# Attention scores on two 64-row halves of TensorE's array, and a written order on all engines from the gate columns to the end of the attention

## Chip, cores and metric

One core of a Trainium2 chip. The time is the device time of one execution in microseconds. Names of engines: PE is TensorE (its weight loads are PEld), DVE is VectorE, ACT is ScalarE, POOL is GpSimd; SP issues most DMAs.

## What is computed

Two layers of a backbone over 1024 latent and 256 context tokens of 1024 channels. Layer 0 (recurrent heads beside Fourier groups) isn't touched. Layer 1 is multi-head latent attention with 16 heads; a head's queries and keys have 64 plain and 32 rotary dimensions, the rotary key is the same for all heads, and the 1024 latent queries see all 1280 keys:

```python
def attend(q, k, v):
    s = jnp.einsum('bqhd,bkhd->bhqk', q, k, preferred_element_type=jnp.float32) * ATTN_SCALE
    p = jax.nn.softmax(s, axis=-1).astype(v.dtype)
    return jnp.einsum('bhqk,bkhd->bqhd', p, v)
...
    q_l = jnp.concatenate([q_l[..., :QK_NOPE], apply_axial_rope(q_l[..., QK_NOPE:], cos, sin)], axis=-1)
    kr_l = apply_axial_rope(kr_l[:, :, None, :], cos, sin)[:, :, 0]
...
    o_l = blocked_attention(q_l, k_all, v_all).reshape(b_, s_, MLA_WIDTH)
    y_lat = (o_l * jax.nn.silu(g_l)) @ w_out
```

The result is the latent stream after a layer norm, `[1, 1024, 1024]` in float32.

## The kernel before

**Precision.** A product of float32 accuracy is made of three float32r products: each operand is split into `hi` and `lo` of 12 bits, and hi·hi, hi·lo and lo·hi are summed in PSUM (`mm3`, lines 90 to 92; `split`, lines 81 to 87, copies on one engine and subtracts on another). The probabilities times values (`po`) and the row sums are plain float32 products, each of which stands in the trace as two instructions.

**Gate columns** (lines 973 to 994). For each of eight blocks `m` of 128 channels, `in1g` is the product of the gate's weights with the normalised activations, 2 x 8 x 3 products of 512 columns, followed by a sigmoid (ACT) and a product (DVE). Between them, spread over 128 steps, stand the closures of `work`: the weights and rotated queries of heads 0 to 3 (`prep_quad`), the queries and keys of heads 0 and 1 (`prep_pair`), their maximum (`max_pass`) and the values (`prep_v`).

**Attention** (lines 1006 to 1131). Heads go in pairs `p` = 0 to 7, queries in halves of 512, keys in ten tiles `kt` of 128. One step (`attend`) computes for both heads the scores `s` (lines 1021 to 1023: three products over 96 or 97 rows; the 97th row of `Qh` holds the negated maximum of a query and meets ones in `Kh`), the exponential (ACT, line 1025) and the running row sum `ra` (POOL, line 1029). After key tiles 1, 3, 5, 7, 8 and 9 it multiplies up to two tiles of probabilities with values (`po`, line 1034): head `a` writes the column half `64a` of the array. `finish` sums `ra` over partitions (`rp`, line 1059, column halves too), inverts in four pieces (DVE, line 1066), multiplies with the gate and stores.

Beside pair `p`, the next pair is prepared: for odd `p + 1` from the weights at hand, for even `p + 1` after a new `prep_quad` of four heads, which is part of the same list of closures. `ra` in `prep_quad` is one rotation: a product `pra`, then a shuffle, three products or sums and two halves of a split on DVE. `qr` copies rotated queries into rows 64 to 95 of `Qh` and `Ql` (DVE, lines 933 and 934). `max_pass` (lines 951 to 967) makes 16 units of three products (512, 512 and 256 keys) with a maximum on DVE after each; `rows` transposes the maxima and a DMA on POOL's queue puts them into the 97th row of `Qh`. Beside pair 7 the output weights are scaled and split (`wo1_load`, lines 1102 to 1109).

**Order.** All this is traced in the order of the loops, but a scheduler then orders every engine's instructions by its own estimates of costs, so the instructions of a step may stand elsewhere. PSUM has eight banks: four for `m_ps` (maxima and preparation), three for `s_ps`, one for `o_ps`.

Of the kernel before, what the change touches and what calls it, by code (L numbers as in the profile page):

```python
# [13 lines left out]
F32 = mybir.dt.float32  # L14
# [26 lines left out]
PVG = {1: (0,), 3: (1, 2), 5: (3, 4), 7: (5, 6), 8: (7,)}  # L41
PVL = (8, 9)
DK = -1
# [11 lines left out]
MB = 4  # L55
SB = 3
# [3 lines left out]
def _body(ctx, tc, ap, out, dbg=None):  # L60
# [36 lines left out]
    # ---------------------------------------------------------------- constants  # L97
# [13 lines left out]
    # v = 8 softplus(-lambda): softplus(x) = max(x, 0) + log1p(exp(-|x|)),  # L111
    # log1p(e) = 2 atanh(e / (2 + e))
# [26 lines left out]
    # the channel DFT folded into the group weights  # L139
# [9 lines left out]
    # ---------------------------------------------------------------- adaLN  # L149
    # stationary: the silu of the two condition vectors, 32 columns (two used)  # L150
# [8 lines left out]
    # shift and scale of both layers, channel-major: [128, layer, stream, 16] (8 shift, 8 scale)  # L159
# [14 lines left out]
    def ada_units(src, row, nm):  # L174
        """products of one set of four column chunks, a k-tile at a time, summed in SBUF"""
# [25 lines left out]
    def ada_gate(row):  # L201
        # rows 32j + m: chunk j of (layer, half), stream m
# [8 lines left out]
    # layer 0 by quarters of the channels, so that the projection can start on the first  # L211
# [4 lines left out]
    def ada_part(h):  # L216
# [12 lines left out]
        # chunk 2 s + i of shift (s = 0) and scale (s = 1): channel block 2 h + i  # L229
# [82 lines left out]
    # ---------------------------------------------------------------- RG-LRU heads  # L312
# [78 lines left out]
    # x projections run one head pair ahead of the gates that use them  # L391
# [3 lines left out]
    nop = lambda: None  # noqa: E731  # L395
# [18 lines left out]
    # ---------------------------------------------------------------- Fourier channel groups  # L414
# [24 lines left out]
    def fourier(g, work=()):  # L439
        """input projection of one group, then the rest as closures"""  # L440
# [9 lines left out]
        # even and odd parts over the token index, halves 0 .. N/2 - 1  # L450
# [7 lines left out]
        # the latent stream once more about N/4, for even and for odd frequencies  # L458
# [6 lines left out]
        # columns: u_ctx[N/2], ev_lat[N/4] and the alternating sums of both streams  # L465
# [15 lines left out]
        def channel(n, f0, wt):  # L481
            # channel DFT, tokens onto partitions
# [10 lines left out]
        def small():  # L493
# [7 lines left out]
            # alternating terms and bias  # L501
# [13 lines left out]
        def seq(n, tn, nm):  # L515
            # even frequencies in the first half of the columns, odd ones in the second
# [27 lines left out]
        nop = lambda: None  # noqa: E731  # L544
# [29 lines left out]
    def y_load(t, p):  # L574
        """the first eight channel blocks of a token tile"""
# [15 lines left out]
    # ---------------------------------------------------------------- layer 0: output projection, norm  # L591
# [6 lines left out]
    def w1_load(k, p, tag, eh, el):  # L598
        """the small columns of layer 1's input projection, a k-tile"""
# [202 lines left out]
    for n, t in enumerate(TOKE):  # L802
# [8 lines left out]
        if n == WG:  # L811
            wg_load(0, S, G)
# [18 lines left out]
    def slots(p, i0):  # L831
        for i in (i0, i0 + 1):
# [5 lines left out]
            if i == 0:  # L838
                for t in range(NT):
                    G.tensor_copy(out=Kh[0][96:97, P * t : P * t + P], in_=one)  # L840
# [464 lines left out]
```

## Time and profile before

| | us |
|---|---|
| median of three runs | 1495.59 (1495.51 to 1504.29) |
| the profiled execution's own time (its span) | 1498.8 |
| of it up to the gate columns | 722 |
| gate columns | 109 |
| attention, pairs 0 to 6 | 501 |
| attention, pair 7, to the first product of the output projection | 69.5 |
| output projection | 97.3 |

The stretches are read from the timeline: first `in1g`, first `s`, end of pair 6, first `yf`. An engine's busy time counts its instructions, and a PE instruction's duration includes the time through the array; so PE's pace is read from the distance between starts. In the rows, `128*64` is rows times columns of the array in use, and `x8` stands for eight instructions merged into one line.

### The profile page before, as it was taken

What the parts mean: (1) busy time and instruction counts of PE and PEld (TensorE: products, weight loads), DVE (VectorE), ACT (ScalarE), POOL (GpSimd) and SP (SyncE); (2) the same over time, 40 slices, a digit from 0 to 9 for tenths busy, and PEclk for the clock granted to TensorE, in tenths of its full rate; (3) what the DMA queues carried; (4) which work ended last, traced back from release to release, by engine and by line L of the source; (5) the groups of instructions that cost most, each with busy time, mean ns of one, the idle gap of its engine ahead of it and who ended that gap; (6) DMA issues with size and microseconds to landing.
All of it is one profiled execution on the core that took longest, in us unless ns stands there. A gap on an engine that the chain in (4) does not pass through costs nothing.

```text
span 1498.8 us, 18430 instructions
## 1 busy us (share of the span) xinstructions
PE 1434.9 (96%) x6880; PEld 1040.1 (69%) x6880; DVE 1037.0 (69%) x1636; ACT 571.7 (38%) x840; POOL 706.4 (47%) x460
## 2 busy tenths in 40 slices
PE   6998999999999999999999999999999999998898
PEld 3776777778888788879888655655566556554586
DVE  4669778765765243348675769787977787779498
ACT  2276565665113221124321544443444334443110
POOL 1135434343212154213411676677667756689652
PEclk9999999999999999999999999999999989999999
DMA  8613233332304653310231101010100000022542
GB/s 302 229 52 107 99 105 109 109 102 85 111 29 147 211 168 115 119 37 26 95 106 50 60 15 43 15 32 22 36 15 15 29 14 15 15 71 71 181 135 91
DMA packets 63641, 127.05 MB, mean 85 GB/s; under 512 B 5304, under 2 KB 31160, under 8 KB 61248
## 3 DMA queue, kind: packets, MB, share of 16 engines
q1 hardware_dynamic: 60592, 117.82, 24.1%
q0 software_dynamic: 2528, 7.67, 1.4%
q8 instruction: 54, 0.88, 0.3%
q10 hardware_dynamic: 432, 0.39, 0.1%
q14 instruction: 35, 0.29, 0.1%
HBM read 101.14 MB, written 24.66 MB: 84 GB/s over the span
## 4 chain that ended last, share of the span: by engine, by line
PE 72%; DVE 20%; DMA 3%; issue 2%; ACT 2%; POOL 1%; SPq 0%; DVEq 0%; ACTq 0%; POOLq 0%
PE z L272 13%; PE y L651 10%; PE po L1034 8%; PE yf L1167 6%; PE mx L955 5%; PE s L1021 4%; PE s L1023 4%; PE s L1022 4%; PE in1g L92 2%; PE in1g L90 2%; PE in1g L91 2%; DVE xc L322 2%; DVE th L367 1%; DVE gate L372 1%; DVE ri L1066 1%
## 5 line engine op out<-in xcount | busy, mean ns | idle before, releaser
L1029 POOL TENSOR_TENSOR ra<-ra,p 128x512 f32<-128x512 f32 x256 | 351.4, 1399 | 96.2 <-ACT p L1025 95.8
L1025 ACT ACTIVATE p<-s 128x512 f32<-128x512 f32 x320 | 190.1, 597 | 249.9 <-PE s L1023 222.2
L956 DVE TENSOR_REDUCE m<-mx 128x1 f32<-128x512 f32 (+1 forms) x384 | 207.8, 591 | 55.1 <-PE mx L955 53.8
L272 PE MATMUL z<-uh,w0h 128*128 128x512 f32 (+1 forms) x576 | 150.0, 367 | 4.3 <-ACT uh L81 4.3
L87 POOL TENSOR_TENSOR w0l<-w,w0h 128x1024 fp32r<-128x1024 f32 x24 | 63.9, 2664 | 184.5 <-DVE w0h L83 126.4
L272 PE MATMUL z<-uh,w0l 128*128 128x512 f32 (+1 forms) x576 | 147.7, 362 | 0.0
L272 PE MATMUL z<-ul,w0h 128*128 128x512 f32 (+1 forms) x576 | 147.7, 362 | 0.0
L1021 PE MATMUL s<-Qh,Kh 97*128 97x512 f32 x320 | 132.5, 414 | 6.3 <-ACT p L1025 6.3
L1022 PE MATMUL s<-Ql,Kh 96*128 96x512 f32 x320 | 128.1, 400 | 0.0
L1023 PE MATMUL s<-Qh,Kl 96*128 96x512 f32 x320 | 128.1, 400 | 0.0
L955 PE MATMUL mx<-Kh,Qh 96*128 96x512 f32 (+1 forms) x384 | 115.8, 376 | 7.9 <-DVE Ql L87 4.3
L272 PEld LDWEIGHTS z<-uh,w0h 128*128 128x128 f32 x576 | 98.4, 190 | 33.4 <-issue 10.7
L955 PEld LDWEIGHTS mx<-Kh,Qh 96*128 96x128 f32 x384 | 69.4, 190 | 66.2 <-issue 22.6
L272 PEld LDWEIGHTS z<-ul,w0h 128*128 128x128 f32 x576 | 96.7, 190 | 18.7 <-issue 1.0
L272 PEld LDWEIGHTS z<-uh,w0l 128*128 128x128 f32 x576 | 96.5, 190 | 18.4 <-issue 2.0
L350 ACT ACTIVATE gate<-gps,vec 128x512 f32<-128x512 f32 (+1 forms) x96 | 57.5, 616 | 103.6 <-PE gps L92 103.4
L1021 PEld LDWEIGHTS s<-Qh,Kh 97*128 97x128 f32 x320 | 60.9, 190 | 48.3 <-issue 24.9
L1034 PE MATMUL po<-p,v_even 128*64 128x512 f32 x320 | 85.9, 620 | 0.0
L1034 PE MATMUL po<-p,v_odd 128*64 128x512 f32 x320 | 82.7, 615 | 0.0
L1029 POOL TENSOR_TENSOR ra<-p,p 128x512 f32<-128x512 f32 x32 | 48.4, 1533 | 70.6 <-ACT p L1025 70.6
L386 POOL TENSOR_TENSOR gate<-gate,gate 128x1280 f32<-128x1280 f32 x8 | 23.9, 2992 | 112.2 <-DVE gate L383 97.1
L1023 PEld LDWEIGHTS s<-Qh,Kl 96*128 96x128 f32 x320 | 61.7, 193 | 15.7 <-issue 3.2
(357 smaller groups left out, 2983.3 us busy)
## 6 DMA issues: line engine op xcount, KB each, us to landing
w<-in_w SPq DMA_DIRECT2D x24, 512.0 KB, 4.4
adaw<-in_ada SPq DMA_DIRECT2D x32, 256.0 KB, 4.9
adawm<-in_ada SPq DMA_DIRECT2D x8, 1024.0 KB, 5.7
adawg<-in_ada_g SPq DMA_DIRECT2D x8, 1024.0 KB, 4.9
y_dr<-sg SPq DMA_DIRECT2D x10, 640.0 KB, 5.5
woraw<-in_wo SPq DMA_DIRECT2D x12, 512.0 KB, 3.6
xt<-in_x_cm SPq DMA_DIRECT2D x8, 640.0 KB, 6.4
yra<-y_dr SPq DMA_DIRECT2D x10, 512.0 KB, 4.8
```

The costliest lines, as they stand in the source:

```text
L87: el.tensor_tensor(out=lo, in0=src, in1=f(hi), op=ALU.subtract)
L272: TE.matmul(z[:, a : a + n], wi[:, kt, :], ui[kt][:, a : a + n], start=(kt == 0 and ui is uh and wi is wh), stop=(kt == KT - 1 and wi is wl))
L651: TE.matmul(ps[:, 512 * hf : 512 * hf + 512], a[k], b[k][:, 512 * hf : 512 * hf + 512], start=(k == 0 and a is yh and b is woh), stop=(k = ...
L955: TE.matmul(ps[:, :n], Qh[s][0:96, P * t : P * t + P], Kh[s][0:96, a0 : a0 + n], start=True, stop=True)
L956: V.tensor_reduce(out=m3[:, i : i + 1], in_=ps[:, :n], axis=AX.X, op=ALU.max)
L1021: TE.matmul(ps, Kh[s][0:97, ks], Qh[s][0:97, c], start=True, stop=False)
L1022: TE.matmul(ps, Kh[s][0:96, ks], Ql[s][:, c], start=False, stop=False)
L1023: TE.matmul(ps, Kl[s][:, ks], Qh[s][0:96, c], start=False, stop=True)
L1025: S.activation(out=e, in_=ps, func=AF.Exp, scale=SCALE)
L1029: G.tensor_tensor(out=ra, in0=st["e"][0][a] if kt == 1 else ra, in1=e, op=ALU.add)
L1034: TE.matmul(st["o"][64 * a : 64 * a + 64, :], quad[q][6][:, k, 128 * i + 64 * a : 128 * i + 64 * a + 64], st["e"][k][a], start=(k == 0), s ...
L1167: TE.matmul(ps[i], a[:, k, :], b[k][:, pieces[i]], start=(k == 0 and a is oh and b is w1o), stop=(k == 7 and a is ol))
```

## The change

Scores and maxima no longer run over 96 rows. The plain 64 dimensions of both heads of a pair stand in one tile of 128 partitions (`Qh`, `Ql`, `Kh`, `Kl`: head 0 in rows 0 to 63, head 1 in rows 64 to 127), and each head's product uses its 64 rows of the array. The rotary part gets tiles of its own: `KR1` holds the rotary keys' hi and lo parts under each other (64 rows), `R1` the queries' hi part twice; `KR2` and `R2` carry hi·lo in 32 rows and the maximum in a 33rd row. So a head's scores take five products of 64 (or 33) rows instead of three of 96, the two heads' alternate, and both write one PSUM tile of two banks; one `Exp` and one sum cover both heads. A maximum unit covers both heads and one chunk of keys: four products of 64 rows, two maxima.

From the gate columns to the end of the attention, `manual_schedule` keeps PE, DVE, ACT and POOL in the order in which the kernel traces them. The next pair's preparation gets fixed places: `near` right behind a step's scores, `far` at the step's end. `prep_quad` moves to the even pair before (keys 8, 12 and 16 of its 20), `prep_v` stays beside the odd pair. `po` comes at key tiles 3, 5, 7 and 9 in twos; the last two tiles, the row sums and the inversions go into the next half (`finish`). Rotated queries move by DMA on SP instead of DVE copies, and so does the maximum's row. `rp` is copied to SBUF by ACT before it is inverted. In pair 7, POOL and DVE add one head's sum each, and ACT casts the output weights' hi parts. PSUM: three banks for `m_ps`, two tiles of two banks for `s_ps`, one for `o_ps`. Comments are removed, and nothing ahead of the gate columns changes but the split of `wg_load` into a DMA and a split. The core of the diff:

```diff
-    m_ps, m_psc = pool("m_ps", MB, space=PSUM)
-    s_ps, s_psc = pool("s_ps", SB, space=PSUM)
+    m_ps, m_psc = pool("m_ps", 3, space=PSUM)
+    s_ps, s_psc = pool("s_ps", 2, space=PSUM)
...
+    def rotary_keys():
+        for a in range(2):
+            V.memset(f(KR2)[64 * a + 32 : 64 * a + 64, :], 1.0)
+        S.copy(out=KR1[64:96, :], in_=kr_t[64:96, :])
+        V.tensor_tensor(out=KR1[96:128, :], in0=kr_t[64:96, :], in1=f(KR1)[64:96, :], op=ALU.subtract)
+        load(f(KR1)[0:64, :], f(KR1)[64:128, :])
+        for a in range(2):
+            load(f(KR2)[64 * a : 64 * a + 32, :], f(KR1)[64:96, :])
...
         def qr():
             for a in range(2):
                 g = slice(64 * i + 32 * a, 64 * i + 32 * a + 32)
-                V.tensor_copy(out=Qh[sl[a]][64:96, :], in_=f(roth)[g, :])
-                V.tensor_copy(out=Ql[sl[a]][64:96, :], in_=f(rotl)[g, :])
+                for r in range(2):
+                    load(f(R1[b])[64 * a + 32 * r : 64 * a + 32 * r + 32, :], f(roth)[g, :])
+                load(f(R2[b])[64 * a : 64 * a + 32, :], f(rotl)[g, :])
...
-        return [(kn(a0, n), 1.3) for a0, n in CH3] + [(qn(0), 1.5), (qr, 2.2), (qn(1), 1.5)]
+        return [qr] + [kn(a0, n) for a0, n in CH3] + [qn(0), qn(1)]
...
-        def unit(a, t):
+        def unit(t, i):
             def run():
...
+                a0, n = CH3[i]
+                ps = [m_ps.tile([P, 512], F32, tag="m", name=f"mx{p}{t}{i}{a}") for a in range(2)]
+                for q, k, st in ((Qh[b], Kh[b], True), (R1[b], KR1, False)):
+                    for a in range(2):
+                        r = slice(64 * a, 64 * a + 64)
+                        TE.matmul(ps[a][:, :n], q[r, P * t : P * t + P], k[r, a0 : a0 + n], start=st, stop=not st)
+                for a in range(2):
+                    V.tensor_reduce(out=m3s[t][:, a, i : i + 1], in_=ps[a][:, :n], axis=AX.X, op=ALU.max)
+                if i == 2:
+                    V.tensor_reduce(out=nm[:, :, t], in_=m3s[t], axis=AX.X, op=ALU.max)
...
-                G.dma_start(out=Qh[s][96:97, :], in_=row[8 * a : 8 * a + 8, :])
+                load(f(R2[b])[64 * a + 32 : 64 * a + 33, :], f(row)[8 * a : 8 * a + 8, :])
...
+    order = ExitStack()
+    order.enter_context(tc.manual_schedule(engines={e.engine for e in (TE, V, S, G)}))
...
+        b = p % 2
+        ps = s_ps.tile([P, 2, 512], F32, tag="s", name=f"s{p}{hf}{kt}")
+
+        parts = ((Kh[b], Qh[b], 64), (Kh[b], Ql[b], 64), (Kl[b], Qh[b], 64), (KR1, R1[b], 64), (KR2, R2[b], 33))
+        for j, (k, w, n) in enumerate(parts):
+            for a in range(2):
+                r = slice(64 * a, 64 * a + n)
+                TE.matmul(ps[:, a, :], k[r, ks], w[r, c], start=(j == 0), stop=(j == len(parts) - 1))
+        es = at.tile([P, 2, 512], F32, tag="p", bufs=PB, name=f"p{p}{hf}{kt}")
+        S.activation(out=es, in_=ps, func=AF.Exp, scale=SCALE)
+        if kt:
+            ra = st["ra"]
+            for eng, h in ((G, slice(0, 2)),) if p < 7 else ((G, slice(0, 1)), (V, slice(1, 2))):
+                eng.tensor_tensor(out=ra[:, h], in0=(st["e"][0] if kt == 1 else ra)[:, h], in1=es[:, h], op=ALU.add)
...
+        return {1: [rest], 3: [rows], 4: [piece(0)], 5: [piece(1)], 6: [piece(2)], 7: [piece(3)], 8: [last]}
...
+            prep = prep_pair(p + 1)
+            mx = max_pass(p + 1)
+            near[0] += prep[:2]
+            far[0] += prep[2:3]
+            near[1] += prep[3:4]
+            far[1] += prep[4:5]
+            near[2] += prep[5:]
+            at_ = [(g, b) for g in range(2, 2 * NT) for b in range(2) if not (g == 2 and b == 0) and (b == 0 or g % 2)]
+            at_.insert(0, (2, 1))
+            for (g, b), u in zip(at_, mx[:-1]):
+                (far if b else near)[g].append(u)
+            g = at_[len(mx) - 2][0]
+            near[g + 1].append(mx[-1])
+            if p % 2:
+                later = prep_v((p + 1) // 2)
+                for i, u in enumerate(later):
+                    far[4 + 2 * i].append(u)
+            elif p < 6:
+                later = prep_quad(p // 2 + 1)
+                for i, u in enumerate(later):
+                    far[8 + 4 * i].append(u)
...
-                    split(w1o[k], w1p[k], r, V, V)
+                    split(w1o[k], w1p[k], r, S, V)
...
                 attend(p, hf, kt, st)
-                for u in steps[NT * hf + kt]:
+                for u in near[g]:
+                    u()
+                if kt > 2 and kt % 2:
+                    pv(p, st, kt - 3)
+                    pv(p, st, kt - 2)
+                for u in tail.get(kt, ()):
+                    u()
+                for u in far[g]:
                     u()
...
+    order.close()

```

## Rows read from the trace of the kernel before

**Rows 1.** The page's chain that ended last: shares of the span by engine.

```profile
PE 72%; DVE 20%; DMA 3%; issue 2%; ACT 2%; POOL 1%; SPq 0%; DVEq 0%; ACTq 0%; POOLq 0%
```

**Rows 2.** Windows: stretch, its us, then each engine's busy us, PEclk, DMA share, GB/s.

```profile
722.00:831.00 109.00, 109.00 (x504) 90.19 (x503) 66.37 (x140) 29.37 (x52) 28.00 (x23) 1.00 0.27 86
831.00:1332.00 501.00, 491.28 (x2071) 290.98 (x2071) 387.07 (x691) 220.22 (x382) 350.24 (x272) 0.99 0.08 25
1332.00:1401.50 69.50, 57.81 (x212) 27.86 (x210) 57.88 (x38) 27.20 (x46) 65.36 (x37) 0.90 0.30 92
```

**Rows 3.** Timeline of PE in an attention step: start us, us, engine, line, operation.

```profile
1088.80 0.39 PE L1021 MATMUL s<-Qh,Kh 97*128 97x512 f32 x1
...
1089.95 0.39 PE L955 MATMUL mx<-Kh,Qh 96*128 96x512 f32 x1
...
1090.42 0.28 PE L955 MATMUL mx<-Kh,Qh 96*128 96x256 f32 x1
1090.54 0.40 PE L1021 MATMUL s<-Qh,Kh 97*128 97x512 f32 x1
```

**Rows 4.** Timeline of PE where `po` and row sums alternate.

```profile
1092.60 0.64 PE L1034 MATMUL po<-p,v_odd 128*64 128x512 f32 x1
1092.62 0.64 PE L1059 MATMUL rp<-ra,ones 128*64 128x512 f32 x1
1093.08 0.59 PE L1034 MATMUL po<-p,v_odd 128*64 128x512 f32 x1
...
1093.95 0.59 PE L1034 MATMUL po<-p,v_odd 128*64 128x512 f32 x1
```

**Rows 5.** Timeline of PE around one visit to the column halves.

```profile
1079.95 0.39 PE L1023 MATMUL s<-Qh,Kl 96*128 96x512 f32 x1
1080.27 1.94 PE L1034 MATMUL po<-p,v_odd 128*64 128x512 f32 x8
1082.14 1.08 PE L955 MATMUL mx<-Kh,Qh 96*128 96x512 f32 x4
1083.06 0.40 PE L1021 MATMUL s<-Qh,Kh 97*128 97x512 f32 x1
```

**Rows 6.** Waits of PE, pairs 0 to 6: total us, times, longest.

```profile
PE mx L955 <- DVE Ql L87: 4.3, 3, 1.4
PE mx L955 <- DVE ri L1066: 2.3, 3, 0.8
```

**Rows 7.** Waits of PE, last pair.

```profile
PE s L1021 <- ACT p L1025: 6.3, 1, 6.3
PE rp L1059 <- POOL ra L1029: 5.4, 1, 5.4
```

**Rows 8.** Timeline of DVE, first and last operation of one rotation (six in all).

```profile
1045.11 0.74 DVE L890 STREAM_SHUFFLE rot<-pra 128x512 f32<-128x512 f32 x1
...
1050.18 0.69 DVE L87 TENSOR_TENSOR rotl<-rot,roth 128x512 fp32r<-128x512 f32 x1
```

**Rows 9.** Groups by line: shapes, count, busy us, mean ns, idle before.

```profile
L1029 POOL TENSOR_TENSOR ra<-ra,p 128x512 f32<-128x512 f32 x256 | 351.4, 1399 | 96.2 <-ACT p L1025 95.8
L956 DVE TENSOR_REDUCE m<-mx 128x1 f32<-128x512 f32 (+1 forms) x384 | 207.8, 591 | 55.1 <-PE mx L955 53.8
```

**Rows 10.** Timelines of PE and of DVE at the end of the attention.

```profile
1401.58 0.74 PE L1167 MATMUL yf<-w1oh,oh 128*128 128x512 f32 x2
...
1401.68 3.39 DVE L1066 RECIPROCAL ri<-rp 128x128 f32<-128x128 f32 x4 [0.59 <-PE rp L1059]
```

**Rows 11.** DMA issues: queue, count, KB each, median us to landing.

```profile
rc<-in_ropec_cm SPq DMA_DIRECT2D x8, 256.0 KB, 2.7
...
Qh<-mrow POOLq DMA_DIRECT2D x16, 4.0 KB, 1.6
```

**Rows 12.** Groups by line, the output weights' preparation in the last pair.

```profile
L87 DVE TENSOR_TENSOR w1ol<-w1oraw,w1oh 128x1024 fp32r<-128x1024 f32 x8 | 17.0, 2130 | 0.1
...
L83 DVE CAST w1oh<-w1oraw 128x1024 fp32r<-128x1024 f32 x8 | 11.1, 1385 | 0.1
```

More of the change, by code (lines that the diff above doesn't have):

```diff
@@ L911, in run @@
             return r
-        return [(run(t), 0.8) for t in range(0, NT, 2)]
+        return [run(t) for t in range(0, NT, 2)]
     def prep_pair(p):
@@ L925, in run @@
                     mm3(pq, wh[:, k, i, :], wl[:, k, i, :], qnh[k][:, c], qnl[k][:, c], k == 0, k == 1)
-                for a in range(2):
-                    split(Qh[sl[a]][0:64, c], Ql[sl[a]][0:64, c], pq[64 * a : 64 * a + 64, :], S, V)
+                split(Qh[b][:, c], Ql[b][:, c], pq, S, V)
             return run
@@ L965, in rows @@
             for a in range(2):
-                s = 2 * (p % 2) + a
-                G.dma_start(out=Qh[s][96:97, :], in_=row[8 * a : 8 * a + 8, :])
-        return [(unit(a, t), 2.0) for t in range(8) for a in range(2)] + [(rows, 0.5)]
-    wait = [(lambda: None, 0.0)] * WT
+                load(f(R2[b])[64 * a + 32 : 64 * a + 33, :], f(row)[8 * a : 8 * a + 8, :])
+        return [unit(t, i) for t in range(8) for i in range(3)] + [rows]
+    slots(pr_p, 0)
+    order = ExitStack()
+    order.enter_context(tc.manual_schedule(engines={e.engine for e in (TE, V, S, G)}))
+    nop = lambda: None
     work = prep_quad(0)
-    work = (work[:1] + wait + [(lambda: trq(TOKE[-1]), 0.0), (lambda: slots(pr_p, 0), 0.0)] + wait[:W2]
+    work = (work[:1] + [nop] * WT + [lambda: trq(TOKE[-1]), rotary_keys] + [nop] * W2
             + work[1:] + prep_pair(0) + max_pass(0) + prep_v(0))
@@ L978, in _body @@
         if m + 1 < 8:
-            with tc.issue_after(ends[TOKE[-2]]):
-                wg_load(m + 1, S, G)
+            wg_dma(m + 1)
         wh, wl = wgs.pop(m)
+        sp = s_ps.tile([P, 2, 512], F32, tag="s", name=f"in1g{m}")
         for q in range(2):
-            ps = s_ps.tile([P, 512], F32, tag="s", name=f"in1g{m}{q}")
+            ps = sp[:, q, :]
             c = slice(512 * q, 512 * q + 512)
+            if q and m + 1 < 8:
+                wg_split(m + 1, S, G)
             for k in range(KT):
                 mm3(ps, wh[:, k, :], wl[:, k, :], u1h[k][:, c], u1l[k][:, c], k == 0, k == KT - 1)
-                for u, _ in spread(work, 128, step):
+                for u in spread(work, 128, step):
                     u()
@@ L1014, in attend @@
             st["o"] = o_ps.tile([P, 512], F32, tag="o", name=f"po{p}{hf}")
[L1015 removed]
+            st["ra"] = at.tile([P, 2, 512], F32, tag="ra", bufs=2, name=f"ra{p}{hf}")
             st["e"] = []
[L1017 to L1029 removed]
@@ L1030, in attend @@
-        st["e"].append(es)
-        def pv(k):
-            for a in range(2):
-                TE.matmul(st["o"][64 * a : 64 * a + 64, :], quad[q][6][:, k, 128 * i + 64 * a : 128 * i + 64 * a + 64],
-                          st["e"][k][a], start=(k == 0), stop=(k == NT - 1), tile_position=(0, 64 * a))
-        if pend and kt == DK:
-            pend.pop()()
-        for k in PVG.get(kt, ()):
-            pv(k)
-        if kt == NT - 1:
-            def rest():
-                for k in PVL:
-                    pv(k)
-                st["osb"] = at.tile([P, 512], F32, tag="osb", bufs=2, name=f"osb{p}{hf}")
-                S.copy(out=st["osb"], in_=st["o"])
-            pend.append(rest)
-            if p == 7 and hf or DK < 0:
-                pend.pop()()
+        b = p % 2
```

127 lines of the change are left out of this document (49 added, 78 removed).

## Prediction

> **What bounds the kernel now.** I read the page's chain first: 72% of it is TensorE (PE), 20% VectorE (DVE) [rows 1]. The span was then cut into the stretches that the change touches [rows 2]: the gate columns (109 us), the seven head pairs 0 to 6 of the attention (501 us), and the last pair with what follows it until the output projection starts (69.5 us). PE is busy for 109.0 of 109 and 491 of 501 us. A busy PE need not be at its peak, so I go by the distance between starts. In a stretch of the attention five 512-column products start in 1.15 us, 0.23 each, and a 256-column one takes 0.12 [rows 3]. With these two paces the gate columns add up: 384 products of the columns x 0.23 = 88.3, 16 maximum units of (2 x 0.23 + 0.12) = 9.3, preparation of pair 0 10.9; sum 108.5 of 109. So that stretch is PE alone.
>
> The seven pairs: 140 key steps (7 pairs x 2 halves x 10). A step has six score products, 1.38 us, and four float32 `po` instructions. Two on different column halves start 0.02 apart, and from 1093.08 to 1093.95 two such slots pass, 0.43 each [rows 4], so a step's `po` take 0.86. 140 x 2.24 = 313.6; row sums 14 x 0.86 = 12; maxima 7 x 16 x 0.58 = 65; queries and keys 7 x 4.5 = 31.5; rotated queries 3 x 2.8 and values 3 x 3.6 = 19. Sum 441.
>
> What is missing are visits to the column halves. From the start of the last score product (1079.95) to the next score product (1083.06) 3.11 us pass [rows 5]. Inside are one product (0.23), eight `po` instructions in four slots (4 x 0.43 = 1.72) and four maximum products (3 x 0.23 + 0.12 = 0.81), 2.76 in all. Going there and back costs 0.35. The loops visit seven times in a half (keys 1, 3, 5, 7, 8, 9 and the row sums), 14 x 7 = 98 visits, 34 us. Sum 475 of 501. Of the other 26 us the waits name under 10, among them 4.3 and 2.3 for DVE's queue [rows 6].
>
> The last pair is different. PE needs 20 x 2.24 + 2 + 14 x 0.35 = 52 of 69.5 us; DVE is busy for 57.9, POOL for 65.4, and the granted clock averages 0.90 [rows 2]. PE waits 5.4 us for POOL's sums and 6.3 us for ScalarE (ACT) [rows 7].
>
> **The change, part by part.** *Scores.* Before, a step's two heads take six 96-row products one after the other. After, each head has five of 64 rows, and the two heads stand on different row halves. No row half occurs in this trace. If two run at once, a step costs 5 x 0.23 = 1.15, if not, 2.30. The nearest row is that of column halves, which start 0.02 apart [rows 4]; I take 1.15. Pairs 0 to 6: 140 x 0.23 = -32.2 us. (Pair 7 would have -4.6, but it isn't bound by PE, below.)
>
> *Maximum.* For 128 queries and both heads: before six products (two of them of 256 columns), 1.16; after, two parts in side-by-side halves, 2 x (0.23 + 0.23 + 0.12) = 1.16. No gain, and no loss if two weight loads fit beside 256 columns (0.12); if they were in series, at most 64 x 0.23 = 15 us.
>
> *Changes of the array's division.* Scores and maxima now use row halves, `po` and row sums column halves, and preparation and gate products the whole array. Column visits fall to five per half (key 1, 3, 5, 7, 9; the row sums join key 3's): 14 x 5 - 1 = 69. New are visits to the whole array: per pair keys 0, 1 (another one beside `rest`), 2 and 18, so 28; rotated queries 3 x 2 = 6; values 3 x 5 = 15. 118 instead of 98. In the gate columns 24 maximum units of row halves stand singly between whole-array products: 24 visits where there were none. What a change between whole array and row halves costs isn't in this trace. It lies between 0 (products of 96, 97 and 128 rows follow each other at 0.23 [rows 3]) and the 0.35 of a column visit [rows 5]. I take 0.35: the operands of two heads stand in the array at once, as in the column case. Pairs +20 x 0.35 = +7.0; gate columns +24 x 0.35 = +8.4. By the lower end 24 + 49 = 73 visits are free, which is 26 us less.
>
> [...]
>
> *Queues in the written order.* PE, ACT, DVE and POOL no longer let a ready instruction pass a waiting one. PE's danger is a maximum unit that waits for one of three `m` buffers, which DVE empties. In pairs 0, 2 and 4 the next quad's rotation is now at keys 12 and 16. One rotation holds DVE for 5.8 us (1045.11 to 1050.87) [rows 8]. At keys 12 to 18 DVE has 2 x 5.8 of it, a third of a pair's reductions (207.8/8 = 26 [rows 9], so 8.7), and one normalising, about 5 (3.4 of reciprocals [rows 10]): 25.3 us. PE has there 7 x 1.15 + 3.1 (maxima) + 5.2 (`po`) + 0.9 + 2.8 + 5 x 0.35 = 21.8. The excess of 3.5 plus a wait for the first buffer is about 5 us a pair, 15 us; another 3 us for buffers elsewhere. The 10 us that the waits show now (they too stand beside the rotations, in odd pairs) go. Net +8; bounds: 0 waits (-10) and double my waits (+26).
>
> *Covered work.* Copies of rotated queries leave DVE and become six DMAs of 128 KB a pair on SP. They are issued at key 0, and the first use is the maximum at key 2, about 9 us of PE work later. A transfer of 256 KB on SP lands in 2.7 us [rows 11]; uncovered, it would cost that once a pair. The maximum's row goes from POOL's queue to SP's and has all of key 19 (3 us) against 1.6 us to landing [rows 11]. Splits on 128 instead of 2 x 64 partitions halve ACT's and DVE's share there. One `Exp` over 1024 columns replaces two of 512; ACT is busy 220 of 501 us [rows 2], so this gives nothing. Nor does POOL's wider sum (two of 1.40 before [rows 9]; at most 25 us a half beside 32 us of PE).
>
> *Last pair.* DVE gives the cast of `w1oh` to ACT (8 x 1.39 = -11.1 [rows 12]) and takes one of two sums, 18 of 512 columns. Nearest row: the subtraction of 1024 columns beside POOL, 2.13 [rows 12], so 1.07 x 18 = +19. 57.9 - 11 + 19 = 66; with POOL's sums halved DVE's two-input operations should shorten by some 10%, and I take 60. PE (20 x 2.01 + 2 + 11 x 0.35 = 46) is below that. The end gets longer: now the projection starts at 1401.58 while DVE still inverts [rows 10]; after, the first split of `ol` stands behind four reciprocals (3.4), two products and itself (some 2.6): 6 us, plus 1 for the last row sums. 60 + 7 = 67 against 69.5: -3, with bounds of 46 + 7 = 53 (-17) and 72 (+3).
>
> **Sum.** Gate columns +8.4; pairs 0 to 6: -32.2 + 7.0 + 8 = -17.2; end -3. Together -11.8 us on the profiled execution's 1498.8. That one stands 3.2 us over the median of 1495.59; on the median 1484.
>
> **Rivals.** *A: changes between rows and whole array are free.* For it: different row counts follow each other without a gap. Against it: row halves carry two products at once. -26 us: 1458.
>
> *B, slower: the halves do not run quite side by side.* Place: each pair of row halves, 800 in the scores and 384 in the maxima. From 0.01 us more per pair (0.24) the 11.8 us are gone, and from 0.023 more on it is slower by over 1%. If the 0.02 by which the second half starts later [rows 4] is not hidden under the next pair, a pair costs 0.25: +24, 1508; two weight loads in series, each as long as a 256-column product with its load (0.12 [rows 3]), come to 0.24; no overlap at all to +258. For it: each half needs a 128-column weight load of its own within 0.23. Against it: the column halves do keep their 0.43.
>
> [...]
>
> *C: the written order waits more than the old one.* If DVE's queue holds PE in all seven pairs as I expect it in three, and the last pair gives +3: +26 us: 1510.
>
> *D: the last pair becomes PE's.* -14 more: 1470; it goes with any of the others.
>
> **How the numbers follow.** Forecast 40% (own range 1466 to 1499), A 26%, B 20%, C 14%; D is inside the forecast's and A's spread. A measurement of this kernel can tell about 1%, 15 us, from no change. Faster by over 1% (below 1481): 0.15 of the forecast's 0.40 and A, 0.41. Slower by over 1% (above 1510): 0.12 of B's 0.20 and half of C, 0.19. Within: 0.40. The range leaves out the lower third of A (combined with D) and the upper half of B: 1448 to 1522.
>
> **What would show it.** Right: in the timeline two `s` products on the two row halves start within 0.03 us and pairs follow at 0.23; the windows show pairs 0 to 6 in some 484 us and the gate columns in some 117; beside each lone maximum unit in the gate columns a third of a microsecond is missing; PE's waits stand at the rotations. Wrong: gate columns at 109 (A); a pair of halves over 0.24 (B); PE idle for DVE in odd pairs, or for a DMA into `R1` or `R2` (C); a last pair near 53 us (D).

## The result and the profile after

The changed kernel takes 1556.6 us, the kernel before 1498.4 us in the runs beside it: 1.0374 times as long, interval 1.034 to 1.0408. One of the four executions of the changed kernel took 2990.8 us; it counts in the median, not in the ratio. The forecast was 1484, its range ended at 1522. In the profiled executions (1553.7 and 1498.8 us) the loss lies in three stretches, and in each of them the forecast missed (its column takes the prediction's own 109, 501 and 69.5 us and adds the terms):

| stretch | before | forecast | after | missed by |
|---|---|---|---|---|
| up to the gate columns | 722.2 | 722.2 | 725.6 | 3.4 |
| gate columns | 108.9 | 117.4 | 141.9 | 24.5 |
| pairs 0 to 6 | 500.6 | 483.8 | 509.8 | 26.0 |
| pair 7 to the first `yf` | 69.9 | 66.5 | 77.2 | 10.7 |
| output projection | 97.2 | 97.2 | 99.2 | 2.0 |

Windows of the profile after, for the three rows of [rows 2]: stretch, us, then the busy us of PE, PEld, DVE, ACT and POOL, the granted clock (PEclk), DMA share, GB/s.

```profile
725.60:867.50 141.90, 123.44 (x549) 89.28 (x549) 60.16 (x110) 24.23 (x38) 20.35 (x9) 0.96 0.25 80
867.50:1377.30 509.80, 481.18 (x2959) 282.44 (x2958) 344.93 (x571) 187.29 (x219) 308.65 (x131) 0.95 0.11 34
1377.30:1454.50 77.20, 57.21 (x302) 25.83 (x300) 58.07 (x52) 31.64 (x35) 29.83 (x20) 0.90 0.27 83
```

PE was busy for all of the gate columns before; now it is idle for 18.5 us of them. In pairs 0 to 6 it is idle for 28.6 us (before 9.7), and its granted clock is 0.95 (before 0.99). PE's waits in the three stretches, total us, times, longest, where [rows 6, 7] stood before:

```profile
PE in1g L85 <- DVE sg L1010: 18.5, 8, 7.0
...
PE mx L966 <- DVE m L968: 28.5, 12, 4.2
...
PE s L1041 <- ACT p L1043: 14.5, 7, 3.6
PE yf L1194 <- ACT oh L76: 5.5, 1, 5.5
```

What the forecast says of the two row halves holds. The timeline of PE shows both merged into one line (`x2`) that lasts as long as one product (0.39), and the pairs follow at 0.23 us, where a single 96-row product took 0.23 before [rows 3]:

```profile
1392.80 0.39 PE L1041 MATMUL s<-Ql,Kh 64*128 64x512 f32 x2
1393.03 0.40 PE L1041 MATMUL s<-Qh,Kl 64*128 64x512 f32 x2
```

**The wait in the gate columns.** Timelines of PE, ACT and DVE at the longest of the eight:

```profile
745.45 0.40 PE L87 MATMUL in1g<-u1h,wgl 128*128 128x512 f32 x1
752.81 0.79 PE L85 MATMUL in1g<-u1h,wgh 128*128 128x512 f32 x1 [6.96 <-DVE sg L1010]
...
745.88 0.60 ACT L1009 ACTIVATE sg<-in1g 128x512 f32<-128x512 f32 x1 [3.58 <-PE in1g L87]
...
748.25 2.71 DVE L899 TENSOR_TENSOR rot<-rot,rc 128x512 f32<-128x512 f32 x1
...
752.07 0.68 DVE L1010 TENSOR_TENSOR sg<-sg,in1g 128x512 f32<-128x512 f32 x1
```

The second half's first product follows the first half's last one after 7.36 us. Both halves stand in one PSUM tile `sp` of two banks, and PE enters it again only when ACT's sigmoid and DVE's product of the first half have read it. Here DVE's product also stands behind a rotation.

**A wait in pairs 0 to 6.** DVE, POOL and PE in pair 4, where the weights of the next four heads are prepared beside the maxima of pair 5:

```profile
1195.85 2.49 DVE L1081 TENSOR_TENSOR sgt<-ri,sgt 128x512 f32<-128x512 f32 x1
1200.02 1.91 DVE L78 CAST wkh<-wk 128x512 fp32r<-128x512 f32 x1
...
1195.42 2.37 POOL L1047 TENSOR_TENSOR ra<-ra,p 128x1024 f32<-128x1024 f32 x1 [0.70 <-DVE m L968]
1199.72 1.92 POOL L82 TENSOR_TENSOR wql<-wq,wqh 128x768 fp32r<-128x768 f32 x1 [1.94 <-issue]
...
1198.03 0.38 PE L966 MATMUL mx<-Kh,Qh 64*128 64x256 f32 x1
1202.58 0.38 PE L966 MATMUL mx<-Kh,Qh 64*128 64x256 f32 x1 [4.17 <-DVE m L968]
```

DVE's product ends 0.55 us after POOL's sum, its cast 0.29 us after POOL's subtraction: each lasts until the POOL instruction beside it has ended, and then a little. The maxima stand behind them, PE behind the maxima. The granted clock is 1.00 from 1195 to 1198 us and, behind this wait, 0.51 from 1203.2 to 1206.5. All but 0.6 of the 28.5 us of waits stand in pairs 0, 2 and 4 (8.9, 9.6 and 9.4), which take 79.6, 83.0 and 83.0 us; pairs 1, 3 and 5 take 67.2 to 67.3.

**The wait in pair 7.** ACT, DVE and PE:

```profile
1395.47 1.04 ACT L76 CAST w1oh<-w1oraw 128x1024 fp32r<-128x1024 f32 x1 [4.89 <-DVE w1oraw L1129]
1396.42 1.93 ACT L1043 ACTIVATE p<-s 128x1024 f32<-128x1024 f32 x2
...
1393.42 0.94 DVE L1077 RECIPROCAL ri<-ri 128x128 f32<-128x128 f32 x1
1394.29 1.16 DVE L1129 TENSOR_TENSOR w1oraw<-w1oraw,g1bc 128x1024 f32<-128x1024 f32 x1
...
1397.50 0.53 PE L1041 MATMUL s<-Qh,Kh 64*128 64x512 f32 x2 [3.60 <-ACT p L1043]
```

ACT's cast of the output weights stands ahead of the Exp and waits for DVE's product, which stands behind an inversion. PE waits for the Exp. DVE is no steady bound either: of the 77.2 us it works 58.1 and waits for ACT in turn. Waits of ACT and DVE in pair 7:

```profile
ACT w1oh L76 <- DVE w1oraw L1129: 32.1, 8, 4.9
...
DVE ra L1047 <- ACT p L1043: 9.9, 3, 6.0
DVE w1ol L82 <- ACT w1oh L76: 8.9, 8, 1.1
```

### The profile page after: what moved, and what is told of

Same layout as the page of the kernel before. It is cut to its first block, busy times and chain, and to the rows that moved or that the text cites. A ratio compares the mean times of both kernels' runs of the same rounds, so it can differ in the third digit from the quotient of the medians.

```text
span 1553.7 us, 19795 instructions
## 1 busy us (share of the span) xinstructions
PE 1442.4 (93%) x7904; PEld 1031.4 (66%) x7904; DVE 989.1 (64%) x1507; ACT 541.3 (35%) x664; POOL 622.3 (40%) x288
## 4 chain that ended last, share of the span: by engine, by line
PE 70%; DVE 19%; issue 3%; DMA 3%; ACT 3%; POOL 1%; SPq 0%; DVEq 0%; POOLq 0%; ACTq 0%
PE s L1041 12%; PE z L267 10%; PE y L646 10%; PE po L1053 8%; PE mx L966 6%; PE yf L1194 6%; PE in1g L85 2%; PE in1g L87 2%; PE in1g L86 2%; DVE xc L317 2%; DVE th L362 1%; DVE gate L367 1%; DVE m L968 1%; DVE gate L378 1%; DVE ra L1047 1%
## 5 line engine op out<-in xcount | busy, mean ns | idle before, releaser
L1047 POOL TENSOR_TENSOR ra<-ra,p 128x1024 f32<-128x1024 f32 (+1 forms) x128 | 292.6, 2286 | 174.5 <-ACT p L1043 169.7
L1043 ACT ACTIVATE p<-s 128x1024 f32<-128x1024 f32 x160 | 163.4, 1024 | 266.5 <-PE s L1041 265.3
L267 PEld LDWEIGHTS z<-uh,w0h 128*128 128x128 f32 x576 | 98.8, 191 | 33.4 <-issue 10.7
L966 PE MATMUL mx<-Kh,Qh 64*128 64x512 f32 (+1 forms) x384 | 89.6, 414 | 28.6 <-DVE m L968 28.5
L1041 PE MATMUL s<-R,KR 33*128 33x512 f32 (+1 forms) x640 | 110.4, 414 | 0.0
L1041 PE MATMUL s<-Qh,Kh 64*128 64x512 f32 x320 | 76.4, 455 | 14.5 <-ACT p L1043 14.5
L1041 PEld LDWEIGHTS s<-R,KR 33*128 33x128 f32 (+1 forms) x640 | 69.4, 198 | 12.4
L966 PE MATMUL mx<-KR,R 64*128 64x512 f32 (+1 forms) x384 | 77.7, 366 | 0.0
L85 PE MATMUL in1g<-u1h,wgh 128*128 128x512 f32 x128 | 54.4, 425 | 20.4 <-DVE sg L1010 18.5
L1041 PE MATMUL s<-Qh,Kl 64*128 64x512 f32 x320 | 70.0, 414 | 0.0
L1041 PE MATMUL s<-Ql,Kh 64*128 64x512 f32 x320 | 69.6, 412 | 0.0
```

Source lines behind the costliest of these rows:

```text
L85: TE.matmul(o, lh, rh, start=start, stop=False)
L267: TE.matmul(z[:, a : a + n], wi[:, kt, :], ui[kt][:, a : a + n], start=(kt == 0 and ui is uh and wi is wh), stop=(kt == KT - 1 and wi is wl))
L966: TE.matmul(ps[a][:, :n], q[r, P * t : P * t + P], k[r, a0 : a0 + n], start=st, stop=not st)
L1041: TE.matmul(ps[:, a, :], k[r, ks], w[r, c], start=(j == 0), stop=(j == len(parts) - 1))
L1043: S.activation(out=es, in_=ps, func=AF.Exp, scale=SCALE)
L1047: eng.tensor_tensor(out=ra[:, h], in0=(st["e"][0] if kt == 1 else ra)[:, h], in1=es[:, h], op=ALU.add)
```

## The experiments

The medians of the kernel before were 1498.5 to 1501.1 us in the groups of runs below. Theories and rivals are those of the expectations.

### The gate columns' tile

```diff
-        sp = s_ps.tile([P, 2, 512], F32, tag="s", name=f"in1g{m}")
...
-            ps = sp[:, q, :]
+            ps = s_ps.tile([P, 2, 512], F32, tag="s", name=f"in1g{m}{q}")[:, 0, :]
```

> The changed kernel, but in the gate columns each half of 512 queries has a PSUM tile of its own instead of one tile of two banks for both. Theory: the second half's first product waits for sigmoid and product of the first half because both stand in one tile (PE waits 18.5 us for DVE's sg, eight times); with two tiles the gate columns fall from 142 to about 122 us and the time by 19 to 21 us, to about 1536. Rival: the waits are ACT's and DVE's written order, whatever the tile; then the waits stay or move to the next block and the time falls by less than 5 us.

Measured: 1528.8 us, 1.0206 (1.0178 to 1.0235). The window of the gate columns:

```profile
724.50:842.80 118.30, 118.27 (x548) 87.39 (x548) 60.03 (x110) 24.25 (x38) 20.48 (x9) 1.00 0.29 95
```

That is 28 us off, more than the theory gave. In the profiled executions 23.6 of it lies in this window (141.9 to 118.3), more than the wait itself, because the clock comes back with it (1.00 against 0.96); the rest, some 5 us, is spread over stretches that the edit doesn't touch. PE is busy throughout, and 118.3 us is 0.9 over the forecast's 117.4. The preparation's products take as long as before (in the traces of before and after the 512-column ones stand 0.23 to 0.24 us apart in these columns); what is added, 9.4 us, stands around the 24 lone maximum units, where starts are 0.32 to 0.34 us apart instead of 0.23. That is 0.39 us a visit against the forecast's 0.35. The shared tile is nearly the whole miss: 18.5 us of waiting, and 5.2 us of longer PE instructions (123.44 - 118.27) at the lower clock, 0.96.

### The written order

```diff
-    order.enter_context(tc.manual_schedule(engines={e.engine for e in (TE, V, S, G)}))
```

> The changed kernel without the written order (the scheduler orders all engines as before); the row halves and all else stay. Theory (the loss lies in waits of the written order): waits in the gate columns, beside the rotations and in pair 7 shrink; 1505 to 1530 us. Rival (the loss lies in the row halves and the visits they add, whatever the order): 1545 to 1560 us.

> The kernel before with nothing but the written order on TensorE, VectorE, ScalarE and GpSimd from the gate columns to the end of the attention; full-row scores, four one-bank buffers and three pair buffers as before. Theory: the written order as such costs little where the buffers let the engines run ahead, since the changed kernel without it took the same time: 1490 to 1512. Rival: written order in this kernel costs by itself, because VectorE, ScalarE and GpSimd then wait in the order of the text for one another: 1520 to 1560.

Measured: the changed kernel without the order 1556.5 us, 1.0384 (1.0355 to 1.0414); the kernel before with it 1586.1 us, 1.0588 (1.0551 to 1.0625). The theories for both runs were wrong. The first time lies in its rival's range, but not for the rival's reason, since the stretches trade places. Without the order, the scheduler fills the gate columns (122.4 us, no wait for `sg`), but pairs 0 to 6 go up to 534.0, with this wait of PE above all:

```profile
PE mx L966 <- DVE m L968: 38.9, 30, 2.0
```

The kernel before with the order keeps its gate columns (108.9), and pairs 0 to 6 rise from 500.6 to 579.9. Its largest wait of PE, of 54 us in all:

```profile
PE mx L955 <- DVE Ql L87: 31.2, 7, 5.9
```

DVE and PE in the timeline at one of them, from the last of four copies on:

```profile
1013.89 1.77 DVE L934 CAST Ql<-rotl 32x1024 fp32r<-32x1024 f32 x1
1015.68 1.64 DVE L1063 TENSOR_TENSOR sgt<-sgt,osb 128x512 f32<-128x512 f32 x1
1017.35 0.68 DVE L87 TENSOR_TENSOR Ql<-pq,Qh 64x512 fp32r<-64x512 f32 x1
...
1019.52 0.55 PE L955 MATMUL mx<-Kh,Qh 96*128 96x256 f32 x1 [4.78 <-DVE Ql L87]
```

The copies of rotated queries stand ahead of the query's split, and PE waits for it. The change turned these copies into DMAs. So neither part has a price of its own: the order costs 87 us in the text of before and nothing in the text of after (pairs 24 us better, gate columns 20 worse). The halves with their places cost 58 us without the order (1498.5 to 1556.5) and save 29.5 with it (1586.1 to 1556.6).

### VectorE beside GpSimd in pairs 0 to 6

The sum in two instructions, the casts on another engine, and the sums left out:

```diff
-            for eng, h in ((G, slice(0, 2)),) if p < 7 else ...
+            for eng, h in ((G, slice(0, 1)), (G, slice(1, 2))) if p < 7 else ...
```

> The changed kernel, but POOL adds the two heads' row sums in two instructions of 512 columns instead of one of 1024. Theory: a DVE operation with SBUF operands waits until POOL's running instruction ends (512-column operations take 2.24 to 2.49 us beside the 2.29 us sums, 0.69 alone); with sums of 1.3 us they take at most about 1.9, PE's waits beside the rotations shrink, and the time falls by 6 to 15 us. Rival: DVE simply has too much work there and its operations stay as long on average; within 3 us, or slower because POOL's total grows by 0.3 us a step.

```diff
-            split(wh, wl, w, V, G)
+            split(wh, wl, w, S, G)
...
-            split(kh, kl, u, V, G)
+            split(kh, kl, u, S, G)
...
-                split(roth[:, c], rotl[:, c], st[hf], V, V)
+                split(roth[:, c], rotl[:, c], st[hf], S, V)
```

> The changed kernel, but the casts of the next four heads' preparation (roth, wqh, wkh) are on ACT instead of DVE. Theory: these casts (2.46 us and 1.91 us beside POOL) stand ahead of the maxima that PE waits for in pairs 0, 2 and 4; without them PE's three waits a pair (10 us) roughly halve: 10 to 20 us less. Rival: ACT then waits in its written order for DVE's operands ahead of an Exp and PE waits for ACT instead: within 5 us.

```diff
-        if kt:
+        if kt == 1 and p < 7:
+            G.tensor_scalar(out=st["ra"], in0=st["e"][0], scalar1=1.0, scalar2=None, op0=ALU.add)
+        elif kt and p == 7:
```

> The changed kernel without GpSimd's running sums of the exponentials in pairs 0 to 6: one instruction of the same width stands in each half instead of nine, so the denominators are left out and only the time is read. Theory: VectorE's casts and products on SBUF operands are late because each waits until GpSimd's 2.3 us instruction ends; without these TensorE's waits for VectorE's maxima fall from 28.5 to under 12 us, the clock goes back to 0.98, and pairs 0 to 6 fall from 509.8 to 470 to 490: 1517 to 1537. Rival: VectorE's own queue order makes the maxima late, GpSimd has no part: less than 8 off (1549 to 1557).

Measured: two instructions 1552.6 us, 1.0368 (1.0342 to 1.0394); casts on ACT 1522.3, 1.0163 (1.014 to 1.0186); no sums 1516.6, 1.0114 (1.0083 to 1.0145). Groups by line on DVE (count, busy us, mean ns), first of after:

```profile
L1072 DVE TENSOR_TENSOR sgt<-sgt,osb 128x512 f32<-128x512 f32 x12 | 22.9, 1908 | 0.0
L78 DVE CAST roth<-rot 128x512 fp32r<-128x512 f32 x6 | 14.7, 2457 | 0.2
L82 DVE TENSOR_TENSOR rotl<-rot,roth 128x512 fp32r<-128x512 f32 x6 | 4.2, 692 | 0.2
```

With the sum in two:

```profile
L1072 DVE TENSOR_TENSOR sgt<-sgt,osb 128x512 f32<-128x512 f32 x12 | 13.3, 1112 | 0.0
L82 DVE TENSOR_TENSOR rotl<-rot,roth 128x512 fp32r<-128x512 f32 x6 | 9.8, 1634 | 0.2
L78 DVE CAST roth<-rot 128x512 fp32r<-128x512 f32 x6 | 8.2, 1375 | 0.2
```

Without sums:

```profile
L1074 DVE TENSOR_TENSOR sgt<-sgt,osb 128x512 f32<-128x512 f32 x13 | 8.9, 682 | 0.0
L78 DVE CAST roth<-rot 128x512 fp32r<-128x512 f32 x6 | 2.6, 427 | 0.2
```

The casts on ACT gave 34 us, more than either side had expected; the run without sums gave 40, and its waits and its stretch are within the theory's bounds. Without POOL's sums the same cast takes 0.43 us instead of 2.46. The window of pairs 0 to 6 with the casts on ACT:

```profile
865.70:1343.40 477.70, 464.02 (x2959) 268.90 (x2958) 327.24 (x559) 194.31 (x231) 308.50 (x131) 0.99 0.12 36
```

The same window without sums:

```profile
867.60:1340.20 472.60, 460.75 (x2959) 267.77 (x2958) 305.40 (x571) 187.45 (x219) 48.38 (x20) 1.00 0.12 37
```

PE's wait without sums:

```profile
PE mx L966 <- DVE m L968: 10.1, 9, 2.4
```

The two runs agree on the cause. The same 2959 PE instructions take 460.8 us at a granted clock of 1.00; in the changed kernel there are 20.4 us more of PE time at a granted clock of 0.95 (481.18 - 460.75) and 28.5 us of waiting, together 509.7 of 509.8. Either mend takes most of both away: with the casts on ACT PE is idle for 13.7 us, without sums for 11.9, and the clock is back at 0.99 and 1.00. The sum in two gave at most 4 us, less than the theory's 6 to 15, and the intervals of the two ratios overlap; PE's waits for the maxima stay at 27.4. The rotation's cast falls from 2.46 to 1.38 us, and the subtraction behind it rises from 0.69 to 1.63, which the author puts down to POOL's second instruction; together 3.15 before, 3.01 after.

> The kernel before with the six casts of the next heads' weights and rotations on ScalarE instead of VectorE, nothing else. Theory: the casts cost 34 us in the changed kernel because its maxima run on three buffers used two at a time; before, with four used one at a time, TensorE waited only 9.5 us in pairs 0 to 6, so at most that is won: 1490 to 1499. Rival: the casts are dear in either kernel: 1465 to 1485.

The same move of the casts in the kernel before gives nothing: 1500.7 us, 1.0007 (0.9992 to 1.0023). That is 2 us over the theory's range and far from the rival's, so the casts are not dear in the kernel before. Why they are in the changed one, by its three buffers used two at a time as the theory says or by their place in the written order, no run parts.

### Both mends

> The changed kernel with both mends at once: a PSUM tile of its own for each half of a gate column, and the six casts of the next heads' weights and rotations (roth, wqh, wkh) on ScalarE instead of VectorE. Theory: the two causes are separate, one stands before the first score and one after it, so their gains add: 27.0 + 34.2 = 61 off, 1495 to 1500, which is where the kernel before stands; gate columns about 118 us, pairs 0 to 6 about 478. Rival: both act through VectorE's lateness, so that one mend takes part of the other's gain: 1505 to 1520.

Measured: 1501.2 us, 1.0015 (1.0002 to 1.0029). The stretches add as expected (gate columns 118.3, pairs 0 to 6 477.8); the whole lies 1 us over the range.

### Pair 7

The output weights in three steps of the loop, as lines of the list `far`:

```diff
-                far[2 + 2 * k].append(wo1_load(k))
+                far[1 + 2 * k].append(wo1_load(k))
+                far[2 + 2 * k].append(wo1_hi(k))
+                far[3 + 2 * k].append(wo1_lo(k))
```

> The changed kernel, pair 7's preparation of the output weights in three steps of the loop instead of one: VectorE's product with the gate in step 1 + 2k, ScalarE's cast in step 2 + 2k, VectorE's subtraction in step 3 + 2k. Theory: in pair 7 ScalarE's cast stood ahead of the Exp in the written order and waited for VectorE's product, and TensorE waited 14.5 us for the Exp; with the product a step earlier that wait goes, and pair 7 falls from 77.2 to 65 to 70 us, the whole by 7 to 12 (1545 to 1550). Rival: VectorE has more to do in pair 7 than the pair lasts, so that the order of its work moves the wait elsewhere: less than 3 off (1553 to 1557).

> The changed kernel with four mends: tiles of their own in the gate columns, the six casts on ScalarE, pair 7's output weights in three steps with both sums of pair 7 on GpSimd, and the load and split of the output projection's first tile written ahead of the last head's division. Theory: 1556.6 - 27 - 34 - 8 to 12 in pair 7 - 0 to 6 at the end = 1477 to 1488, faster than the kernel before by over 1%. Rival: ScalarE, which has the casts now, and GpSimd, with both sums, set pair 7 instead, and the end stays: 1492 to 1505.

Measured: the three steps alone 1550.7 us, 1.0342 (1.0314 to 1.0371); all mends 1494.7, 0.9972 (0.9953 to 0.9991). Pair 7 goes from 77.2 to 71.7 and 71.9 us, so the product one step earlier is worth 5.5 of the 10.7 us, less than the theory's 7 to 12. The kernel with all mends misses the theory's range by 7 us and lies in the rival's; PE still waits 10.9 us for the Exp in its pair 7. The fourth mend gave nothing that the trace shows: the load of the projection's first tile is issued only 2.0 us after the store of pair 7's first half (1391.75 and 1389.70), and the projection takes 99.5 us. The next run takes POOL's sums out of pair 7:

> The kernel with all mends, without GpSimd's running sums in pair 7 (one instruction of the same width stands in each half instead of nine; the denominators of pair 7 are left out, only the time is read). Theory: in pair 7 VectorE's sixteen products and subtractions of 1024 columns run at 3.4 us instead of 1.2 because each waits for GpSimd's sum, and ScalarE's casts and Exp wait behind them; without the sums pair 7 falls from 71.9 to 58 to 64, so 1481 to 1487. Rival: ScalarE's own order of casts and Exp sets the pair: less than 3 off (1491 to 1496).

Measured: 1473.7 us, 0.9817 (0.9787 to 0.9846); pair 7 takes 50.4 us, less than the theory gave. DVE's costliest group in pair 7 of the kernel with all mends, sums included:

```profile
L1128 DVE TENSOR_TENSOR w1oraw<-w1oraw,g1bc 128x1024 f32<-128x1024 f32 x8 | 24.3, 3041 | 6.6 <-DMA w1oraw<-in_wo 6.6
```

The window of pair 7 there:

```profile
1325.90:1397.80 71.90, 56.33 (x303) 25.72 (x301) 59.35 (x29) 31.77 (x36) 54.52 (x20) 0.89 0.29 89
```

The same group without sums:

```profile
L1130 DVE TENSOR_TENSOR w1oraw<-w1oraw,g1bc 128x1024 f32<-128x1024 f32 x8 | 9.8, 1221 | 6.9 <-DMA w1oraw<-in_wo 6.9
```

The window without sums:

```profile
1324.30:1374.60 50.30, 48.43 (x302) 24.54 (x300) 29.43 (x29) 31.53 (x36) 8.12 (x4) 1.00 0.41 128
```

ACT's casts and Exps stand in the same order in both, so that order alone isn't the bound. DVE's products last through POOL's sums (3.04 us each against 1.22; the subtractions 2.15 against 1.24, where the theory had 3.4 for both); without sums PE no longer waits for the Exp, and the pair is PE's.

### The price of a visit

On the kernel with all mends, `po` in fours (after keys 5 and 9) and one at a time (after keys 2 to 9):

```diff
-                if kt > 2 and kt % 2:
-                    pv(p, st, kt - 3)
-                    pv(p, st, kt - 2)
+                if kt in (5, 9):
+                    for k in range(kt - 5, kt - 1):
+                        pv(p, st, k)
```

> The kernel with all mends, with the values taken in after steps 5 and 9 in fours instead of after steps 3, 5, 7 and 9 in twos, so that 28 of the visits with column tiles in pairs 0 to 6 fall away (four in pair 7). Theory: a visit costs 0.35 us, in and out, as forecast: 28 x 0.35 = 9.8 off, up to 1.4 more in pair 7, so 1483 to 1488. Rival A: the changes are free or hidden, within 3 of 1494.7. Rival C': four column blocks in a row let ScalarE run dry, and TensorE waits for its Exp afterwards: over 1498.

> The kernel with all mends, with the values taken in one at a time after each of the steps 2 to 9, so that 56 visits with column tiles are added in pairs 0 to 6 (eight in pair 7). Theory: 56 x 0.35 = 19.6 more, and up to 2.8 in pair 7: 1512 to 1518. Rival A: the changes are free or hidden behind the pace of ScalarE: within 5 of 1494.7.

Measured: fours 1536.6 us, 1.0241 (1.0212 to 1.027); singles 1521.8, 1.0139 (1.0106 to 1.0173). The window of pairs 0 to 6 with all mends:

```profile
846.50:1325.90 479.40, 465.70 (x2959) 270.53 (x2958) 327.28 (x559) 194.15 (x231) 308.34 (x131) 0.99 0.12 36
```

Window with fours:

```profile
847.50:1369.30 521.80, 483.30 (x2959) 279.96 (x2958) 328.04 (x559) 193.77 (x231) 311.85 (x132) 0.96 0.11 35
```

PE's wait with fours:

```profile
PE mx L966 <- DVE m L968: 34.3, 30, 2.9
```

Window with singles:

```profile
847.60:1350.60 503.00, 482.11 (x2959) 261.11 (x2958) 331.98 (x559) 193.71 (x231) 309.20 (x131) 0.99 0.11 35
```

PE's wait with singles:

```profile
PE mx L966 <- DVE m L968: 17.3, 25, 1.6
```

Singles add 56 visits and 23.6 us, 16.4 of it PE's busy time at the same clock, the rest waits. Counted in the trace, 32 of the 56 visits stand next to whole-array products and add one change of the array's division instead of two, so there are 80 changes more: 0.20 us each, 0.41 for a visit in and out. The changes aren't free. Singles came out 4 us over the range, for these waits. Fours were a miss by 50 us, on two counts. The row sums, which had joined key 3's visit, made one of their own, so only 15 visits fell away, not the 28 that I wrote. And the visits seem to have been cover: with fewer of them between the maximum units PE reaches the next unit before DVE has emptied a buffer. That is argued from PE's waits, 34.3 us in 30 against 11.9 in 16 with all mends. The time is in the range of rival C', but there is no wait for the Exp among PE's.

### VectorE's divisions on GpSimd

```diff
-            V.tensor_tensor(out=st["sg"], in0=st["sg"], in1=st["osb"], op=ALU.mult)
+            (G if p < 7 else V).tensor_tensor(out=st["sg"], in0=st["sg"], in1=st["osb"], op=ALU.mult)
...
-            V.tensor_tensor(out=st["sg"], in0=st["ri"], in1=st["sg"], op=ALU.mult)
+            (G if p < 7 else V).tensor_tensor(out=st["sg"], in0=st["ri"], in1=st["sg"], op=ALU.mult)
```

> The kernel with all mends, with the two products per half that divide the values (gate by sum, and by the reciprocal) on GpSimd instead of VectorE in pairs 0 to 6. Theory: on VectorE they took 2.2 and 1.5 us, stretched beside GpSimd's sums, and the maxima behind them were late; on GpSimd they queue behind the sums and VectorE is free of 48 us: TensorE's waits for the maxima fall from 11.9 to under 6 us, and the whole to 1486 to 1491. Rival: the rest of the waits comes from the rotation and the weights in even pairs, or GpSimd's sums come late instead: 1493 to 1500.

Measured: 1487.4 us, 0.9908 (0.9874 to 0.9941), the fastest of the kernels that compute all of it. The window of pairs 0 to 6:

```profile
843.90:1316.60 472.70, 460.87 (x2957) 268.01 (x2956) 287.90 (x533) 194.32 (x231) 337.46 (x156) 1.00 0.12 36
```

The time falls within the theory's range, but the waits for the maxima only from 11.9 to 10.0 instead of under 6: 4.8 us of the gain is PE's busy time at the higher clock (1.00 against 0.99). The other 10 us of waits stand in pairs 0, 2 and 4; what makes them wasn't followed.

## Why the prediction was wrong, point by point

- **Scores (-32.2) and changes of division (+7.0, +8.4): right.** Pairs of row halves follow at 0.23, the gate columns came within 1 us of the forecast once their tile was split, and a visit costs 0.39 us there and 0.41 in the run with singles, against 0.35. PE's busy time in pairs 0 to 6 without sums, 460.8 us, is 5 under the forecast's (491.3 - 32.2 + 7.0). Rivals A and B, on which most of the chance stood beside the forecast, both fell: neither was the halves' pace the trouble nor were the changes free. B's 0.25 for a pair (1508 us) wasn't reached: the second half starts 3 ns after the first (median). (For A the prediction cites [rows 3] for 128-row products too; the rows show 96 and 97 alone. Those of 128 rows stand 0.23 apart in the gate columns of before, 731.55 and 731.78.)
- **Gate columns: a step left out, 24.5 us.** The step counted products and visits, but not what the two-bank tile holds back. Before, each half had a tile of its own; the change's new `s_ps` tile made the half's epilogue part of PE's path. It stands in the code, not in the trace of before: a change of a tile's shape had to be followed to every user of the pool, the gate columns too.
- **Queues in the written order: under-sized, 26 us.** The step put the late maxima beside the next heads' preparation in pairs 0, 2 and 4, where they are, at about 5 us a pair; they were 8.9 to 9.6. It priced POOL's 1024-column sum at nothing for POOL and forgot what it does to DVE: casts and products on SBUF wait through it (the rotation's cast 2.46 us beside it, 0.43 without). 28.5 us of waits stood there against a forecast of 18 (the 10 of before and 8). That alone lies inside the step's own bound (+26); the clock behind the waits, 20.4 us at 0.95, had no term. PE's own work was some 5 us less than forecast. In pairs 1, 3 and 5 PE doesn't wait, as forecast.
- **The order itself: not a term to be priced alone.** Rival C named waits for DVE's queue in all seven pairs and about 1510 us; the waits stood in three. In the text of after the order costs nothing, in the text of before 87 us.
- **Pair 7: the wrong path, 10.7 us.** The forecast let the pair last as long as DVE's work, 60 us. The work had that size, 58.1 us, but DVE itself stood waiting. No run shows the 10% by which the step shortened DVE's operations beside halved sums: the subtraction of 1024 columns took 1.23 us against 2.13 before, the product with the gate 1.45 against 2.05, and DVE's own sums 1.22 instead of the 1.07 taken. The cast's move was booked as 11 us off DVE, without naming what is queued behind it on ACT: ACT waits 32.1 us in its casts for DVE's products, and the Exp, DVE and PE behind them. A product one step earlier gave 5.5 us; the rest of the 10.7 wasn't parted in this kernel. In the kernel with all mends, where POOL adds both heads, the sums hold the pair at 71.9 instead of 50.4 us. Rival D (the pair becomes PE's) is true only without the sums.
- **The end: 6 us, right in size, not in cause.** PE waits 5.5 us for the split of `oh`, but the trace puts ACT's delay down to the load of `orw` (3.68 us), not to the inversions of the last half. The load is issued at 1449.39, 2.0 us after the store of the first half's last product.
- **The 3.4 us ahead of the gate columns** weren't forecast. 1.9 of them are a wait of the first `in1g` for ACT's copy of `kr_t`; the rest wasn't followed.

## What to carry to other kernels

When a change alters a tile's shape or a buffer's count, list every user of that pool and ask what each now waits for; a shared two-bank tile chained its two halves here (18.5 us of waits). In a written order, price what stands ahead of the instruction that empties PE's buffers, with its duration beside the other engine's longest instruction, not its duration alone (the rotation's cast took 2.46 us beside POOL's sums and 0.43 without). A saving on PE is worth its size only while the engines that feed it keep up; here PE's waits in pairs 0, 2 and 4 cost twice, once as idle time (28.5 us in all) and once as PE time at a lower clock (20.4 us, at 0.95).

## What the runs showed of the hardware

- **DVE's casts and products on SBUF last longer beside POOL's sums.** The rotation's cast of 128x512 took 2.46 us beside sums of 1024 columns, 1.38 beside sums of 512 and 0.43 without. Not all of DVE's work is held: the maxima of 512 columns, which read PSUM, took 680 ns with the sums and 681 without, and the inversions of 128 columns 943 ns both times. A chain of two DVE operations gained little from shorter POOL instructions: beside sums of 512 columns the cast and the subtraction behind it took 3.01 us together, beside sums of 1024 columns 3.15.
- **PE's lower clock shows in the distances of products.** After 5.46 us of idle time the granted clock is 0.50, and products of 512 columns stand 0.43 us apart (two in 0.85), where they stand 0.23 apart at a granted clock of 1.00 (pair 1, 947.1 to 1014.4). Window and timeline of PE at the start of the output projection:

```profile
1454.50:1457.80 3.30, 3.29 (x8) 2.65 (x9) 3.04 (x3) 1.05 (x1) 0.00 (x0) 0.50 0.22 56
...
1454.51 1.22 PE L1194 MATMUL yf<-w1oh,oh 128*128 128x512 f32 x2 [5.46 <-ACT oh L76]
1455.53 1.06 PE L1194 MATMUL yf<-w1ol,oh 128*128 128x512 f32 x2
1456.38 1.06 PE L1194 MATMUL yf<-w1oh,ol 128*128 128x512 f32 x2
```

- **Two row halves cost one.** In pair 1 of the changed kernel the second half of a score pair starts 3 ns after the first (median), and the next pair 0.23 us after it, the pace of a single product; maxima of 512 columns show nearly the same pace (0.24). Each half had a weight load of its own (2958 loads for 2959 products in pairs 0 to 6).
- **A change of the array's division cost about 0.2 us.** 48 changes between row halves and the whole array lengthened the gate columns by 9.4 us (0.20 each), 80 more changes PE's busy time in pairs 0 to 6 by 16.4 (0.20 each).
